# The second half of the latents' columns as one block of 800 columns, 4 of its 16 row pairs in seven products

## The chip, the cores and the metric

The kernel runs on one core of one Trainium2 chip. The metric is the device time of one execution in microseconds (us). The kernel before took 1927.89 us (median of 3 runs, 1927.67 to 1929.81).

## What is computed

One encoder layer on 256 tokens with 4096 features, in float32:

```python
h = rms_norm(x, g_mix)
proj = einsum('bsd,de->bse', h, w_in)
c_q, c_kv, k_rope, gate_a, q_b, k_b, v_b, gate_b = split(proj, split_idx)
q_a = einsum('bsr,re->bse', rms_norm(c_q, g_q_latent), w_uq)
kv = einsum('bsr,re->bse', rms_norm(c_kv, g_kv_latent), w_ukv)
# dense attention on q_a, kv and the rotated k_rope; windowed attention on q_b, k_b, v_b;
# both gated, w_out, residual; then a gated embedding through w_ple and w_ple_gate; a last rms_norm
```

The change concerns the first 1600 columns of `w_in`: 1024 of the query latent `c_q`, 512 of the key and value latent `c_kv`, and 64 of the rotary key `k_rope`. The kernel calls them the latents. After them come 2048 columns of the gate `gate_a`.

## The kernel before

**Products.** The 256 tokens are two tiles of 128, and the 4096 features are 32 row blocks of 128. Each float32 operand is held as a high and a low part, and each product of a 128x128 piece of x with a row block of weights is three matmuls (`mm`, lines 133 to 135: high by high, high by low, low by high). A row block of weights is loaded by SyncE into a buffer `raw` (4 of them, `RAW`), ScalarE writes its high part `hi` (line 115), and VectorE subtracts it for the low part `lo` (line 116).

**Steps.** All products stand in one list `steps`, and the loop at the end of the program goes through it. In round i it emits the loads and conversions of the steps ahead (`fetch`, `convert`), the matmuls of step i, and then one turn of every running task (`advance`). How far conversions go ahead is set by the ring of `hi`/`lo` buffers: a step with the ring `WP` of three buffers has two further steps converted, a step with a longer ring five (line 1470, `tiles`). All engines take their instructions in the order in which they were emitted. A task is a generator; a `yield` ends its turn. `hook(n, f)` calls f ahead of step n.

**The latents (steps 0 to 63).** They are four chunks of 400 columns (line 1159), 16 steps each; a step takes two row blocks, that is 12 matmuls of 400 columns. At the end of a chunk `done_a(i)` scales the two token tiles out of PSUM into `c_tok` (line 335 on VectorE, 337 on ScalarE), squares the columns for the norms on ScalarE (347), and `turn_c` transposes finished groups of 256 columns through PSUM and splits them into `cT` (316, 125, 127). Chunk 3 spawns `latents`, which copies and rotates the rotary key on GpSimd (370, 212 to 215), transposes it (379), and sets the flag `kpe`; its last turn computes the norms and sets the flag `latents`, for which the steps of `w_uq` and `w_ukv` wait. The banks of PSUM are named m0 to m3, s, o, t0 and t1; the chunks use m0/m1 and m2/m3 in turn, and transposes take t0 and t1 in turn (`turn_bank`).

**Blocks.** The first 1024 columns of the gate, and other wide matrices, are a `Block`: two halves of 512 columns by two token tiles. A pair of row blocks is done either plainly (two steps `c` of 12 matmuls, 24 in all), or by a form of Strassen's scheme (four steps `s` of 3, 6, 6 and 6 matmuls, 21 in all) with seven products instead of eight. The latter needs four differences of weights on VectorE (820) and four sums of x for the pair (`add_sums`, 858 with the splits 115 and 116). `weave(fast, lead, trail)` gives the order of the steps: `lead` plain ones, then the pairs spread among plain ones, then `trail` plain ones. After the last `s` the task `mid` (here `gates_mid`) combines four of the eight PSUM banks, and after the last step `done` (`gates_done`) adds the other four. The gate's block is `weave(range(7), 8, 2)`: 7 of 16 pairs in seven products. Its sums, `x0_sums`, come from a task that is spawned at step 24 (line 1224) and makes the sums of one pair in every four turns, with buffers T2 and T3.

At steps 0 to 15 x is loaded, transposed and split; at step 24 the task `rotary_tables` is spawned, which computes angles on VectorE (181 to 197) and their sine and cosine on ScalarE (200 to 203).

Of the kernel before, what the change touches and what calls it, by code (L numbers as in the profile page):

```python
# [18 lines left out]
P = 128  # L19
# [59 lines left out]
def encoder_layer(ctx: ExitStack, tc: tile.TileContext, x, p, positions, g_mix, w_in, g_q_latent, w_uq,  # L79
# [242 lines left out]

    def done_a(i):
        def task(ps):
            if i == 0:
                yield from x_stats()
                for t in range(NT):
                    c_tok.append(slot(f"B{t}", [OFF_GA]))
                qh, ql = slot("B4", [8, S], F32R), slot("B5", [8, S], F32R)
                kv = slot("B6", [2, 4, S], F32R)  # L330
                cT["q"], cT["kv"] = (qh, ql), (kv[:, 0], kv[:, 1])
            for t in range(NT):
                dst = c_tok[t][:, 400 * i:400 * (i + 1)]
                if t:
                    nc.vector.tensor_scalar(dst, ps[t], rx[:, t:t + 1], None, op0=ALU.mult)
                else:
                    nc.scalar.activation(dst, ps[t], AF.Copy, scale=rx[:, t:t + 1])
            yield
            if i == 3:
                spawn(latents())  # L340
            ends = [400 * i, min(400 * (i + 1), Q_LORA + KV_LORA)]
            if ends[0] < Q_LORA < ends[1]:
                ends.insert(1, Q_LORA)
            for lo, hi in zip(ends, ends[1:]):
                c = 4 if lo == Q_LORA else 5 if lo > Q_LORA else i
                for t in range(NT):
                    nc.scalar.activation(junk[:, :hi - lo], c_tok[t][:, lo:hi], AF.Square,
                                         accum_out=sums[:, c, t:t + 1])
                    yield
            while i and ("cT", i - 1) not in flags:  # L350
                yield
            yield from turn_c(((0,), (1, 2), (3,), (4, 5))[i])
            flags.add(("cT", i))
            if i == 3:
                tot = stat(2 * NT)
                q, kv = tot[:, :NT], tot[:, NT:]
                nc.vector.tensor_tensor(q, sums[:, 0], sums[:, 1], op=ALU.add)
                nc.vector.tensor_tensor(kv, sums[:, 4], sums[:, 5], op=ALU.add)
                nc.vector.tensor_tensor(q, q, sums[:, 2], op=ALU.add)
                nc.vector.tensor_scalar(q, q, KV_LORA / Q_LORA, None, op0=ALU.mult)  # L360
                yield from rsqrt_mean(rqkv, tot, KV_LORA)
                nc.vector.tensor_scalar(rqs, rq, (NOPE + ROPE) ** -0.5, None, op0=ALU.mult)
                flags.add("latents")
        return task
# [292 lines left out]
    def d_mid(key, blk):  # L657
        def task():
            tags = D_TAGS[key]
            if len(tags) == 2:  # L660
                d = [slot(b, [NT, 512]) for b in tags]
            else:
                both = slot(tags[0], [2, NT, 512])
                d = [both[:, 0], both[:, 1]]
            D[key] = d
            if key == ("v", 1):
                E["d"] = slot("T5", [2, NT, S])
                nc.gpsimd.dma_start(E["d"], c_dist)
            ps = blk.ps
            sc = [(rxq if key[0] == "q" else rx)[:, t:t + 1] for t in range(NT)]  # L670

            def add(h, t, m, old):
                nc.vector.scalar_tensor_tensor(d[h][:, t], ps[m], sc[t], old, op0=ALU.mult, op1=ALU.add)

            for t in range(NT):
                nc.scalar.activation(d[0][:, t], ps["M1"], AF.Copy, scale=sc[t])
            for t in range(NT):
                add(1, t, "M6", d[0][:, t])
            add(0, 1, "M7", d[1][:, 1])
            add(1, 0, "M5", d[1][:, 0])  # L680
            add(1, 1, "M5", d[0][:, 1])
            flags.add(("mid", key))
            yield
        return task

    def d_done(key, blk):
        def task():
            d = D[key]
            sc = [(rxq if key[0] == "q" else rx)[:, t:t + 1] for t in range(NT)]
            for m, t, h in (("M2", 0, 0), ("X", 1, 1), ("M3", 0, 1), ("M4", 1, 0)):  # L690
                nc.vector.scalar_tensor_tensor(d[h][:, t], blk.ps[m], sc[t], d[h][:, t], op0=ALU.mult, op1=ALU.add)
            if key == ("v", 1):
# [65 lines left out]
    class Step:  # L758
# [4 lines left out]
        def __init__(self, load, split, run, needs=(), frees=0):  # L763
            self.load, self.split, self.run, self.needs, self.frees, self.after = load, split, run, needs, frees, None
            self.ring, self.flag = WP, None

    Q = 512

    class Block:
# [8 lines left out]

        def __init__(self, w, lhs, sums, name, order, needs, tags, tmp, ring):
            self.w, self.lhs, self.sums, self.name, self.needs, self.tmp = w, lhs, sums, name, needs, tmp  # L780
# [6 lines left out]
        def product(self, m, a, b):  # L787
            first = m not in self.ps
            if first:
                self.ps[m] = bank(self.tags[m], [Q])  # L790
            self.left[m] -= 1
            mm(self.ps[m], a, b, first, self.left[m] == 0)

        def load(self, kt):
            r = wp.tile([P, 2, Q], F32, tag="raw", name=f"raw_{kt}", bufs=RAW)
            nc.sync.dma_start(r.rearrange("p a b -> p (a b)"), self.w[kt * P:(kt + 1) * P, :])
            return r
# [14 lines left out]
        def fast_steps(self, j):  # L812
# [9 lines left out]
            def split1(hi, lo):  # L822
                if isinstance(self.tmp, tuple):
                    T.extend(slot(b, [2, Q]) for b in self.tmp)
                else:
                    both = slot(self.tmp, [4, Q])
                    T.extend((both[:, :2], both[:, 2:]))
# [24 lines left out]
    def add_sums(n, pair, dst, tmp, name, out, rest=0, first=0):  # L852
# [3 lines left out]
        def task():  # L856
# [8 lines left out]
            for j in range(first, n):  # L865
# [12 lines left out]
                for _ in range(1 + rest):  # L878
                    yield
        return task()  # L880


# [96 lines left out]
    P4 = {}  # L979
    WIDE_PLE = {(0, 0): "m0", (0, 1): "m1", (1, 0): "t0", (1, 1): "t1"}  # L980

# [175 lines left out]

    for i in range(4):
        add(from_x(400 * i, 400, done_a(i)))
# [20 lines left out]
    def lay(blk, order, mid, done, ple=None, after=(), used={}):  # L1180
# [5 lines left out]
        for i, key in enumerate(shape):  # L1186
            x = next(step[key])
            x.ring = WP + list(after) if after != () and i > last else blk.ring
            if key == "s":
# [64 lines left out]

    tags = EVEN
    for n, key in enumerate((key, i) for i in range(2) for key in "qkv"):
# [15 lines left out]

    tags = EVEN
    for k in range(WIDE_O):
        hook(len(steps), only(*(("t0", "t1"), ("m0", "m1"), ("m2", "m3"))[k]))
        for h in range(2):
# [6 lines left out]
    for c in (6, 7):  # L1283
        hook(len(steps), lambda c=c: (load_res(c), only("t0", "t1")()))
        if c == 7:
            hook(len(steps) + 6, lambda: spawn(x1_sums()))
            hook(len(steps) + 11, lambda: spawn(load_p()))
        add(Chunk(cols(w_out, 512 * c, 512), 32, 512, lhs_y, ("m2", "m3") if c == 6 else ("m0", "m1"), done_o(c), need_y))
    kept = [("B1",), ("B4",), ("B5",), ("B6",), ("B7a", "T6")]
# [6 lines left out]
    for k in range(WIDE):  # L1296
        order = weave(*((range(6), 6, 4) if k == 0 else (range(7), 4, 4)), 2)
        blk = Block(w_ple_gate[:, 1024 * k:1024 * (k + 1)], lhs_x1, x1_s, "x1_sums", order,
                    lambda kt: [("x1T", kt // 4)], LAST, "B6", WP + ["B4"])
# [3 lines left out]
    tail_banks = {6: (("m0", "m1"), ("t0", "t1")), 7: (("m2", "o"), ("s", "m3")), 8: (("m0", "m1"), ("t0", "t1"))}  # L1303

# [83 lines left out]
    def tiles(i, st):  # L1388
# [11 lines left out]
        seen.append(i)  # L1400
        shape = [st.ch.per, st.ch.n] if isinstance(st, Old) else [2, 512]
        if tag == "wp":
# [124 lines left out]
```

## Time and profile before

| | |
|---|---|
| median of 3 runs | 1927.89 us |
| the profiled execution | 1927.64 us |
| its span, first to last instruction | 1925.9 us |
| matmuls and transposes in the trace | 9272 |
| first matmul of the gate's block | 157.20 us |
| VectorE busy from 175 to 231 us (seven-product pairs of the gate's block) | 55.25 of 56 us |

The profile is one execution; its times are microseconds from its span's start. PE is TensorE's matmul, PEld its weight load, DVE VectorE, ACT ScalarE, POOL GpSimd, SP SyncE. A matmul is listed as longer than the distance to the next, since matmuls overlap in the array; the distance from start to start is what one costs. A group's row gives its line, engine, operation, written tile and read tiles, count, busy time and mean ns of one, and the engine's idle time before it. A row of a wait gives the total, the times and the longest.

### The profile page before, as it was taken

Reading aid. Unit: us, or ns where it says so; the run is one execution under the profiler, and the core shown is the slowest. Engines: PE = TensorE matmul, PEld = TensorE weight load, DVE = VectorE, ACT = ScalarE, POOL = GpSimd, SP = SyncE. Lnnn points to the kernel's source line nnn. Section 1 sums busy time; section 2 is a strip of 40 time slices with the busy share of each in tenths; the row PEclk is TensorE's granted clock in tenths of the full one; section 3 lists DMA queues with packets and bytes.
Section 4 is the critical chain, followed back from the end, with each engine's and each line's share of the span. In section 5 each row is a group of like instructions: output and inputs, shape, how many; then the busy total and the mean of one; then the engine's idle time right before and its main releaser. Section 6 shows DMA issues by size and latency. Waiting matters only on the chain.

```text
span 1925.9 us, 25586 instructions
## 1 busy us (share of the span) xinstructions
PE 1909.8 (99%) x9272; PEld 1626.7 (84%) x9272; DVE 1560.8 (81%) x2162; ACT 1101.3 (57%) x1513; POOL 74.5 (4%) x122
## 2 busy tenths in 40 slices
PE   9999999999999999999999999999999999999997
PEld 8998889998888888888888888888888888888887
DVE  7766966665999999999887778889896698989866
ACT  6555555565555555655556666555565456666643
POOL 1001011220000000000000010000000000000000
PEclk9999999999999999999999999999999999999999
DMA  7676655455666666666664456665666656566675
GB/s 251 188 187 198 196 172 144 145 150 162 188 185 209 209 217 197 209 197 196 218 197 139 135 165 218 201 215 174 230 194 217 189 184 218 186 210 204 207 220 176
DMA packets 147342, 370.59 MB, mean 192 GB/s; under 512 B 12020, under 2 KB 45904, under 8 KB 147216
## 3 DMA queue, kind: packets, MB, share of 16 engines
q1 hardware_dynamic: 145584, 363.90, 61.9%
q0 software_dynamic: 1632, 5.05, 0.7%
q8 instruction: 73, 1.20, 0.3%
q14 instruction: 53, 0.43, 0.1%
HBM read 364.72 MB, written 4.19 MB: 192 GB/s over the span
## 4 chain that ended last, share of the span: by engine, by line
PE 94%; DVE 4%; DMA 1%; issue 1%; ACT 1%; SPq 0%; DVEq 0%; ACTq 0%
PE m L134 20%; PE m L135 20%; PE m L133 20%; PE t L134 4%; PE t L135 4%; PE t L133 4%; PE s L134 3%; PE o L134 3%; PE o L135 3%; PE o L133 3%; PE s L135 3%; PE s L133 3%; DVE lo L116 1%; PE t L445 1%; DVE B L820 1%
## 5 line engine op out<-in xcount | busy, mean ns | idle before, releaser
L116 DVE TENSOR_TENSOR lo<-raw,hi 128x1024 fp32r<-128x1024 f32 (+4 forms) x497 | 549.0, 1109 | 227.6 <-ACT hi L115 225.0
L115 ACT ACTIVATE hi<-raw 128x1024 fp32r<-128x1024 f32 (+4 forms) x497 | 478.4, 967 | 365.9 <-PE m L135 181.2
L133 PE MATMUL m<-hi,Ah 128*128 128x512 f32 (+2 forms) x1130 | 429.2, 380 | 0.0
L134 PE MATMUL m<-lo,Ah 128*128 128x512 f32 (+2 forms) x1130 | 424.6, 376 | 0.9 <-DVE lo L116 0.7
L135 PE MATMUL m<-hi,Al 128*128 128x512 f32 (+2 forms) x1128 | 422.3, 374 | 0.0
L134 PEld LDWEIGHTS m<-lo,Ah 128*128 128x128 f32 x1130 | 212.9, 188 | 34.6 <-DVE lo L116 5.0
L135 PEld LDWEIGHTS m<-hi,Al 128*128 128x128 f32 x1128 | 212.3, 188 | 32.8 <-DVE Al L127 0.2
L133 PEld LDWEIGHTS m<-hi,Ah 128*128 128x128 f32 x1130 | 213.0, 188 | 30.1
L133 PE MATMUL m<-hi,B 128*128 128x512 f32 (+1 forms) x420 | 160.4, 382 | 0.0
L134 PE MATMUL m<-lo,B 128*128 128x512 f32 (+1 forms) x420 | 156.8, 373 | 0.2 <-DVE lo L116 0.2
L135 PE MATMUL m<-hi,B 128*128 128x512 f32 (+1 forms) x420 | 156.7, 373 | 0.0
L115 ACT ACTIVATE hi<-B 128x1024 fp32r<-128x1024 f32 x75 | 79.5, 1061 | 79.9 <-DVE B L820 50.3
L116 DVE TENSOR_TENSOR lo<-B,hi 128x1024 fp32r<-128x1024 f32 x75 | 91.6, 1223 | 4.1 <-ACT hi L115 1.8
L135 PEld LDWEIGHTS m<-hi,B 128*128 128x128 f32 x420 | 78.9, 188 | 11.7
L134 PEld LDWEIGHTS m<-lo,B 128*128 128x128 f32 x420 | 79.1, 188 | 11.3 <-DVE lo L116 0.9
L133 PEld LDWEIGHTS m<-hi,B 128*128 128x128 f32 x420 | 79.0, 188 | 10.6
L115 ACT ACTIVATE B<-raw 128x1024 fp32r<-128x1024 f32 (+1 forms) x66 | 60.5, 925 | 45.8 <-DMA raw<-in_w_in_dram 17.4
L820 DVE TENSOR_TENSOR B<-raw,B 128x512 f32<-128x512 f32 x126 | 86.3, 685 | 0.0
L115 ACT ACTIVATE B<-B 128x1024 fp32r<-128x1024 f32 (+1 forms) x60 | 57.4, 957 | 44.4 <-DVE B L820 22.1
L116 DVE TENSOR_TENSOR B<-raw,B 128x1024 fp32r<-128x1024 f32 (+1 forms) x66 | 69.4, 1059 | 13.5 <-ACT B L115 13.2
L116 DVE TENSOR_TENSOR T<-t,T 128x512 fp32r<-128x512 f32 (+1 forms) x65 | 44.4, 683 | 41.6 <-ACT T L115 41.2
L835 DVE TENSOR_TENSOR lo<-raw,hi 128x1024 fp32r<-128x1024 f32 x57 | 69.5, 1219 | 1.9 <-ACT hi L833 1.8
(780 smaller groups left out, 3774.3 us busy)
## 6 DMA issues: line engine op xcount, KB each, us to landing
raw<-in_w_in_dram SPq DMA_DIRECT2D x320, 512.0 KB, 4.1
raw<-in_w_out_dram SPq DMA_DIRECT2D x128, 512.0 KB, 4.4
raw<-in_w_ple_gate_dram SPq DMA_DIRECT2D x128, 512.0 KB, 4.4
raw<-in_w_in_dram SPq DMA_DIRECT2D x63, 400.0 KB, 3.7
raw<-in_w_uq_dram SPq DMA_DIRECT2D x32, 384.0 KB, 3.5
raw<-in_w_ukv_dram SPq DMA_DIRECT2D x16, 512.0 KB, 3.7
T<-in_x_dram SPq DMA_DIRECT2D x7, 512.0 KB, 6.0
T<-in_x_dram POOLq DMA_DIRECT2D x7, 512.0 KB, 8.2
```

Source lines behind the costliest of these rows:

```text
L115: nc.scalar.activation(hi, src, AF.Copy)
L116: nc.vector.tensor_tensor(lo, src, plain(hi), op=ALU.subtract)
L133: nc.tensor.matmul(ps, ah, bh, start=start, stop=False)
L134: nc.tensor.matmul(ps, ah, bl, start=False, stop=False)
L135: nc.tensor.matmul(ps, al, bh, start=False, stop=stop)
L445: nc.tensor.transpose(tp[:, k, t * P:(t + 1) * P], e[:, t, k * P:(k + 1) * P], ident)
L820: nc.vector.tensor_tensor(dst, a, b, op=ALU.subtract)
L835: nc.vector.tensor_tensor(lo, r[1], plain(hi), op=ALU.subtract)
```

## The change

Chunks 0 and 1 stay. The columns 800 to 1599 become one `Block` with halves of 400 columns, `weave(range(4), 8, 4)`: 4 of 16 pairs in seven products, 40 steps (24 plain ones and 16 of the four pairs). Its `mid` and `done` tasks (`late_mid`, `late_done`) call `half_way` and `all_way`, which are the former bodies of `d_mid` and `d_done`. `late_done` then spawns `latents`, transposes the groups 3, 4 and 5 on the banks o and s, squares, and computes the norms. The sums of x are begun at step 17 instead of 24, one pair in every three turns, with buffers T4 and B7b. The block has a fourth buffer pair, (T6, T5), in its ring, and (T2, T3) after its last pair. The gate's block takes its banks in the order of `follow(EVEN)`, and from there on m0/m1 and m2/m3 are exchanged. `EVEN` is (m0, m1, s, o, m2, m3, t0, t1), and a block's banks stand in the order M2, X, M3, M4, M1, M5, M6, M7.

```diff
@@ turn_c
             split_rows(*(q[:, o:o + 2] for q in cT[key]), tp, G[key][:, o:o + 2])
-            yield
+            if b < 3:
+                yield
@@ done_a: the part for i == 3, the turns (3,) and (4, 5) and the norms go; new tasks
+    def late(h, t):
+        return c_tok[t][:, 800 + 400 * h:1200 + 400 * h]
...
+    def late_mid(blk):
+        def task():
+            half_way(blk.ps, [rx[:, t:t + 1] for t in range(NT)], late)
+            yield
+        return task
...
+    def late_done(blk):
+        def task():
+            all_way(blk.ps, [rx[:, t:t + 1] for t in range(NT)], late)
+            yield
+            assert ("cT", 1) in flags
+            spawn(latents())
+            yield from turn_c((3, 4, 5))
+            for c, lo, hi in ((2, 800, Q_LORA), (4, Q_LORA, 1200), (5, 1200, Q_LORA + KV_LORA)):
+                yield from square(c, lo, hi)
...
+    def half_way(ps, sc, d):
+
+        def add(h, t, m, old):
+            nc.vector.scalar_tensor_tensor(d(h, t), ps[m], sc[t], old, op0=ALU.mult, op1=ALU.add)
+
+        for t in range(NT):
+            nc.scalar.activation(d(0, t), ps["M1"], AF.Copy, scale=sc[t])
+        for t in range(NT):
+            add(1, t, "M6", d(0, t))
+        add(0, 1, "M7", d(1, 1))
+        add(1, 0, "M5", d(1, 0))
+        add(1, 1, "M5", d(0, 1))
+
+    def all_way(ps, sc, d):
+
+        for m, t, h in (("M2", 0, 0), ("X", 1, 1), ("M3", 0, 1), ("M4", 1, 0)):
+            nc.vector.scalar_tensor_tensor(d(h, t), ps[m], sc[t], d(h, t), op0=ALU.mult, op1=ALU.add)
...
-    for i in range(4):
+    for i in range(2):
         add(from_x(400 * i, 400, done_a(i)))
...
-    hook(24, lambda: spawn(add_sums(7, x_pair, z0_dst, ("T2", "T3"), "x0_sums", x0_s, 2)))
+    hook(17, lambda: spawn(add_sums(7, x_pair, z0_dst, ("T4", "B7b"), "x0_sums", x0_s, 1)))
...
+    order = weave(range(4), 8, 4)
+    blk = Block(w_in[:, 800:1600], lhs_x, x0_s, "x0_sums", order, lambda kt: (), EVEN, ("T2", "T3"),
+                WP + [("T6", "T5")], 400)
+    lay(blk, order, late_mid(blk), late_done(blk), after=[("T2", "T3")])
+    hook(len(steps), only("o", "s"))
     order = weave(range(7), 8, 2)
-    blk = Block(w_in[:, OFF_GA:OFF_GA + 1024], lhs_x, x0_s, "x0_sums", order, lambda kt: (), EVEN, ("T2", "T3"),
+    blk = Block(w_in[:, OFF_GA:OFF_GA + 1024], lhs_x, x0_s, "x0_sums", order, lambda kt: (), follow(EVEN), ("T2", "T3"),
                 WP + [("T5", "T6")])
     lay(blk, order, gates_mid(blk), gates_done(blk))
+    hook(len(steps), only("t0", "t1"))
+    M = M[::-1]
```

More of the change, by code (lines that the diff above doesn't have):

```diff
@@ L338, in task @@
             yield
[L339 to L349, printed above, removed]
+            yield from square(i, 400 * i, 400 * (i + 1))
@@ L350, in task @@
             while i and ("cT", i - 1) not in flags:
                 yield
-            yield from turn_c(((0,), (1, 2), (3,), (4, 5))[i])
+            yield from turn_c(((0,), (1, 2))[i])
             flags.add(("cT", i))
[L354 to L363, printed above, removed]
+        return task
@@ L668, in task @@
                 nc.gpsimd.dma_start(E["d"], c_dist)
[L669 to L681, printed above, removed]
+            half_way(blk.ps, [(rxq if key[0] == "q" else rx)[:, t:t + 1] for t in range(NT)], lambda h, t: d[h][:, t])
             flags.add(("mid", key))
@@ L688, in task @@
             d = D[key]
-            sc = [(rxq if key[0] == "q" else rx)[:, t:t + 1] for t in range(NT)]
-            for m, t, h in (("M2", 0, 0), ("X", 1, 1), ("M3", 0, 1), ("M4", 1, 0)):
-                nc.vector.scalar_tensor_tensor(d[h][:, t], blk.ps[m], sc[t], d[h][:, t], op0=ALU.mult, op1=ALU.add)
+            all_way(blk.ps, [(rxq if key[0] == "q" else rx)[:, t:t + 1] for t in range(NT)], lambda h, t: d[h][:, t])
             if key == ("v", 1):
@@ L777, in encoder_layer, with __init__ @@
         NAMES = "M2", "X", "M3", "M4", "M1", "M5", "M6", "M7"
-        def __init__(self, w, lhs, sums, name, order, needs, tags, tmp, ring):
+        def __init__(self, w, lhs, sums, name, order, needs, tags, tmp, ring, q=Q):
+            self.q = q
             self.w, self.lhs, self.sums, self.name, self.needs, self.tmp = w, lhs, sums, name, needs, tmp
@@ L823, in split1 @@
                 if isinstance(self.tmp, tuple):
-                    T.extend(slot(b, [2, Q]) for b in self.tmp)
+                    T.extend(slot(b, [2, self.q]) for b in self.tmp)
                 else:
-                    both = slot(self.tmp, [4, Q])
+                    both = slot(self.tmp, [4, self.q])
                     T.extend((both[:, :2], both[:, 2:]))
@@ L1271, in encoder_layer @@
         add(ch)
-    tags = EVEN
+    tags = LAST
     for k in range(WIDE_O):
-        hook(len(steps), only(*(("t0", "t1"), ("m0", "m1"), ("m2", "m3"))[k]))
+        hook(len(steps), only(*(("t0", "t1"), ("m2", "m3"), ("m0", "m1"))[k]))
         for h in range(2):
```

33 lines of the change are left out of this document (24 added, 9 removed).

## The prediction

> **What bounds the kernel now.** I read the page first, then the waits of TensorE, then the stretches of the changed stage.
>
> ```profile
> span 1925.9 us, 25586 instructions
> PE 1909.8 (99%) x9272; PEld 1626.7 (84%) x9272; DVE 1560.8 (81%) x2162; ACT 1101.3 (57%) x1513; POOL 74.5 (4%) x122
> PEclk9999999999999999999999999999999999999999
> PE 94%; DVE 4%; DMA 1%; issue 1%; ACT 1%; SPq 0%; DVEq 0%; ACTq 0%
> ```
>
> TensorE is busy for 99% of the span, at the full granted clock in all 40 slices, and 94% of the chain that ended last is TensorE. The busy share alone does not say that nothing is lost, because a matmul's end is modelled. The waits say it:
>
> ```profile
> PE m L1456 <- DVE junk L1450: 1.5, 1, 1.5
> PE m L134 <- DVE lo L116: 0.9, 5, 0.2
> PE t L270 <- DMA T<-in_x_dram: 0.9, 1, 0.9
> ```
>
> Apart from the start, matmuls waited for a low part five times, 0.9 us in all. So the time is the number of matmuls by their distance, and a change pays if it removes matmuls and brings no wait. The stages that matter are these:
>
> ```profile
> core 0: us, PE busy (x) PEld busy (x) DVE busy (x) ACT busy (x) POOL busy (x), PEclk, DMA share, GB/s
> 46.00:86.00 40.00, 40.00 (x226) 39.91 (x225) 29.00 (x69) 22.34 (x38) 0.00 (x0) 1.00 0.65 184
> 86.00:155.00 69.00, 68.99 (x386) 68.51 (x385) 45.76 (x71) 35.74 (x57) 0.00 (x0) 1.00 0.71 192
> 175.00:231.00 56.00, 56.00 (x246) 45.52 (x245) 55.25 (x80) 33.05 (x35) 0.00 (x0) 1.00 0.65 202
> ```
>
> The second row is nearly all of chunks 2 and 3, which the change replaces: VectorE has 23 us to spare there. The third row is the seven-product part of the gate's block: VectorE is at 55.25 of 56 us, so that block is the narrow place behind the change.
>
> **What goes from TensorE.** A pair in seven products is 21 matmuls against 24. Four pairs remove 4 x 3 = 12 matmuls of 400 columns; the instruction lists of the two programs agree (12 fewer of 128x400, the same transposes). One costs the distance of starts:
>
> ```profile
> 119.81 0.35 PE L133 MATMUL m<-hi,Ah 128*128 128x400 f32 x1
> 124.88 0.34 PE L134 MATMUL m<-lo,Ah 128*128 128x400 f32 x1
> ```
>
> These are the first and the last of 29 matmuls in a row, 28 distances: 5.07 / 28 = 0.181 us. **12 x 0.181 = 2.17 us less.**
>
> The Trainium skill, in "TensorE: Matmul & The Clock Gate", section "Back-to-back issue gap", gives N / 2.4 + 2.5 ns for an isolated matmul, 169 ns at 400, and about 131 ns at N = 512 for a stream with weight loads. The sum would be 12 x 0.169 = 2.03 us by the first, and under 12 x 0.131 = 1.6 us by the second (estimates from that page). The trace has 0.181 us for 400 columns in just such a stream, so it agrees with neither, and least with the second.
>
> **What VectorE gains in work.** Rows for its prices, all of before:
>
> ```profile
> L116 DVE TENSOR_TENSOR lo<-raw,hi 128x800 fp32r<-128x800 f32 x43 | 42.5, 990 | 28.8 <-ACT hi L115 28.8
> L116 DVE TENSOR_TENSOR lo<-raw,hi 128x1024 fp32r<-128x1024 f32 x3 | 3.7, 1226 | 2.7 <-ACT hi L115 2.7
> L335 DVE TENSOR_SCALAR B<-m,st 128x400 f32<-128x400 f32 x3 | 1.9, 629 | 0.2 <-PE m L135 0.2
> 200.55 0.69 DVE L820 TENSOR_TENSOR T<-raw 128x512 f32<-128x512 f32 x1
> 201.15 0.68 DVE L820 TENSOR_TENSOR T<-raw,raw 128x512 f32<-128x512 f32 x1
> 208.27 0.69 DVE L820 TENSOR_TENSOR T<-raw 128x512 f32<-128x512 f32 x1
> 575.50 2.19 DVE L673 SCALAR_TENSOR_TENSOR B<-t,st,B 128x512 f32<-128x512 f32 x3
> ```
>
> Instructions in a row overlap by about 0.09 us (starts 0.60 us apart at a length of 0.69). A column costs (1226 - 990) / 224 = 1.05 ns. So from start to start a difference of 400 columns costs 0.60 - 112 x 0.00105 = 0.48 us, a low part of 400 the same, one of 800 0.90 us. A scaled addition out of PSUM costs 2.19 / 3 = 0.73 at 512, so 0.61 us at 400 (estimates from these rows). A pair in seven products takes 4 x 0.48 + 0.48 + 3 x 0.90 = 5.1 us of VectorE, against 1.8 us plain: 13.2 us more for four. Evictions are nine scaled additions instead of two (line 335, about 0.54): 4.4 us more. That is 17.6 us on an engine with 23 us free in the stage, and the sums of five pairs leave it besides.
>
> Locally: between two pairs the order is three plain steps and one pair. TensorE needs 57 x 0.181 = 10.3 us for that, VectorE 5.1 + 3 x 0.9 = 7.8 us. In the gate's block the same account is 7.72 us of VectorE (208.27 - 200.55) against 33 matmuls. So the new block hides its work with 2.5 us per group, and I charge **nothing**. If that cover were gone, the price would be as in the gate's block, below: 0.2 us a pair, under 1 us for four.
>
> ScalarE converts 1200 columns more per pair (a high part of 400 and one of 800), some 5 us in all, and has 33 us free in the stage. SyncE's list has the same 32 loads of 400 KB at the same places, so nothing is queued differently there; the DMA engines are busy for 0.71 of the stage.
>
> **The crowd at steps 24 to 31.** The sums begin seven steps earlier, beside the rotary tables.
>
> ```profile
> 74.67 0.98 DVE L116 TENSOR_TENSOR lo<-raw,hi 128x800 fp32r<-128x800 f32 x1
> 75.57 2.04 DVE L191 SCALAR_TENSOR_TENSOR T<-T 128x64 f32<-128x64 f32 x8
> 70.67 0.69 DVE L858 TENSOR_TENSOR T<-Ah,Al 128x512 f32<-128x512 f32 x1
> 71.40 1.02 DVE L858 TENSOR_TENSOR T<-T 128x128 f32<-128x128 f32 x4
> 81.92 0.63 ACT L115 ACTIVATE B<-T 128x512 fp32r<-128x512 f32 x1 [1.32 <-DVE T L858]
> 82.57 1.28 ACT L200 ACT_TABLE_LOAD   x1
> 84.47 1.62 ACT L115 ACTIVATE hi<-raw 128x800 fp32r<-128x800 f32 x2
> 86.05 0.34 PE L133 MATMUL m<-hi,Ah 128*128 128x400 f32 x1
> 86.40 0.45 PE L134 MATMUL m<-lo,Ah 128*128 128x400 f32 x1
> 86.69 0.34 PE L135 MATMUL m<-hi,Al 128*128 128x400 f32 x1
> ```
>
> Before, the ScalarE part of one pair's sums (81.92, waiting for VectorE) stood ahead of the table load (1.28 us) in step 29; the high part behind it came at 84.47, and TensorE lost (86.69 - 86.05) - 2 x 0.181 = 0.28 us. In the new program no sum's part stands ahead of the table load in that step, so I take the **0.28 us** off. What is late next is VectorE: in step 26 the sums of pair 3 (0.73 + 0.94 us) now stand between two low parts together with the eight operations of line 191 (1.96 us). From the low part of step 28 to the end of that of step 29 this is 0.90 + 1.67 + 1.96 + 0.90 = 5.4 us, where two buffers ahead allow 3 x 2.17 = 6.5 us, less the 1 us in which ScalarE makes the high part. The margin is about 0.1 us at steps 29 and 30. I charge **0.1 us**; bounds 0 and 1.7 us (the whole of a sum, 0.73 + 0.94 us, outside the margin).
>
> **The gate's block.** Its waits are VectorE's deficit:
>
> ```profile
> 203.34 0.39 PE L133 MATMUL m<-T,Ah 128*128 128x512 f32 x1
> 203.63 0.50 PE L134 MATMUL m<-T,Ah 128*128 128x512 f32 x1
> 203.97 0.39 PE L135 MATMUL m<-T,Al 128*128 128x512 f32 x1
> 173.77 0.87 DVE L127 SCALAR_TENSOR_TENSOR B<-t,gT,B 128x256 fp32r<-128x256 f32 x2
> 174.89 0.68 DVE L820 TENSOR_TENSOR T<-raw 128x512 f32<-128x512 f32 x1
> 186.08 0.39 PE L135 MATMUL t<-hi,B 128*128 128x512 f32 x1
> 189.94 0.39 PE L134 MATMUL s<-lo,Ah 128*128 128x512 f32 x1
> ```
>
> From 186.08 to 189.94 are 17 distances: 0.227 us at 512 columns. At 203 TensorE lost 0.63 - 2 x 0.227 = 0.18 us; 33 x 0.227 = 7.49 us against VectorE's 7.72 us gives 0.2 us a pair, so it is the deficit, once the conversions ahead are used up. Three of the five waits above are of this kind, some 0.5 us. In the new program the last transpose's splits (173.77, 0.8 us) come two steps earlier and no longer stand before the first difference (174.89). VectorE enters with 0.8 us in hand, about what the pairs lack. The added evictions (four of 0.61 us) and two further splits (0.8 us) fall into the eight plain steps before, 8 x 12 x 0.227 = 21.8 us with 8 x 1.14 = 9.1 us of low parts. Against it: four more squares on ScalarE among the first pairs, and the norms come later. I take **0.3 us** off; bounds 0.5 less and 0.5 more.
>
> **After it** TensorE's list is the same with banks renamed, and six conversions in all move by a place or so in VectorE's list because the rings stand at another position. I charge nothing, bounds -0.3 and +0.5 us.
>
> **Sum:** -2.17 - 0.28 + 0.1 - 0.3 = -2.65 us, on the profiled execution's 1927.64 us: 1925.0 us. Its median is 0.25 us above that, so 1925.2 us.
>
> **Rivals.**
>
> *The new work eats the gain.* The crowd costs its 1.7 us, the four pairs wait 0.2 us each, the gate's block 0.5 us more, and the moved conversions cost 0.5 us: -2.17 + 3.5 = +1.3, which is 1929.2 us by the median; with half of these costs it is 1927.5. For it speaks that VectorE is near its limit on both sides of the new block; against it that each term needs its own margin to fail.
>
> *Slower: TensorE stands at the first transposes of the second half.* They are in its queue after one step of the gate's block, 12 x 0.227 = 2.7 us, and read what `all_way` writes; the whole queue waits behind them. The last of the four evictions can start only after the block's last matmul and takes 0.61 us, so the cover holds until VectorE is some 2 us behind. Were it behind by all the conversions ahead (five of the gate's block, 5 x 1.14) and the five additions of `half_way` (3.1), 8.8 us, the wait would be 6.8 us and the time 1927.9 - 2.2 + 6.8 = 1932.5 us. It decides from 10.3 us of VectorE per group on, against my 7.8: only then does VectorE fall behind at all. The rotary key is another queue there, but a safe one:
>
> ```profile
> 157.51 0.41 POOL L370 COPY T<-B 128x64 f32<-128x64 f32 x2 [151.04 <-ACT B L337]
> 161.66 1.61 POOL L215 TENSOR_TENSOR T<-T,T 128x256 f32<-128x256 f32 x1
> ```
>
> GpSimd needs 163.27 - 157.51 = 5.8 us, and the rotary key's transposes stand in TensorE's list five steps, 13.6 us, after the block's end.
>
> *The change does not do what it says.* The list of instructions shows the 12 matmuls gone; chance nil.
>
> **How the numbers follow.** The forecast has 78%, the eaten gain 14%, the slower one 4%, and 4% is left for more than I count (other waits going too, under 1924 us). About 0.2%, 3.9 us, is what a measurement of this kernel can tell from no change: forecast and eaten gain both lie within it, but for 1% of the forecast. So faster 5%, same 91%, slower 4%. The forecast's own range is 1924.3 to 1926.8, from the terms' better and worse bounds together with the runs' spread; taking in part of the eaten gain, 1924.2 to 1927.5.
>
> **What would show it.** Right: no wait at TensorE over 0.4 us between 10 and 300 us, 12 fewer matmuls of 400 columns, the first matmul of the gate's block at about 154.8 us (157.20 - 2.17 - 0.28 + 0.1), no wait at step 32 behind the table load, and fewer waits in the gate's pairs. Wrong: waits for `lo` in the new block, at its evictions (transposes on o and s), or shifts of more than 0.5 us after the gate's block.

## The result, and the profile after

| | before | after |
|---|---|---|
| median of 21 runs each | 1927.45 us (1926.14 to 1929.81) | 1929.93 us (1928.8 to 1931.78) |
| the profiled execution | 1927.64 us | 1930.17 us |
| its span | 1925.9 us | 1928.4 us |

The ratio after to before is 1.0014, with a 95% interval of 1.0008 to 1.0019. The forecast was 1925.2 us in a range of 1924.2 to 1927.5. So 2.7 us were expected to go and 2.5 us came.

The page of after: the span, TensorE's line, the granted clock, and the shares of the chain that ended last.

```profile
span 1928.4 us, 25605 instructions
PE 1908.9 (99%) x9260; PEld 1623.0 (84%) x9260; DVE 1575.7 (82%) x2193; ACT 1104.2 (57%) x1521; POOL 75.5 (4%) x122
PEclk9999999999999999999999999999999999999998
PE 91%; DVE 6%; DMA 1%; issue 1%; ACT 1%; SPq 0%; DVEq 0%; ACTq 0%
```

The 12 matmuls are gone (9272 to 9260), the granted clock is at 9 tenths or more in every slice but the last (8), and TensorE's share of the chain went from 94% to 91%, VectorE's from 4% to 6%. VectorE holds TensorE up somewhere. The waits of TensorE in after say where (us in total, times, the longest):

```profile
PE m L133 <- DVE B L901: 1.8, 1, 1.8
PE m L134 <- DVE lo L116: 1.5, 8, 0.3
PE m L134 <- DVE T L116: 0.5, 1, 0.5
PE m L133 <- ACT Ah L125: 0.5, 1, 0.5
```

The first row is new and a single wait: TensorE stood for line 901, which is `all_way`. The waits for low parts (line 116) were 0.9 us in all; the second and third row make 2.0, and one for a low part in a buffer B adds 0.2. The last row is at the very start, which the change does not touch.

Not every loss is a row of that table, so I use one more number. **TensorE's excess** is the sum, over all its instructions of a stretch, of the distance to the next start less the median distance of that size in the same execution (0.227 us at 512 columns, 0.180 at 400). The stretch from 0 to 50 us varies from one execution to the next (2.7 to 6.1 us in the runs below, with no edit there), so the later stretches are compared.

| excess, us | whole span | 0 to 50 | 50 to 100 | 100 to 150 | 150 to 200 | 200 to 250 | 500 to 600 |
|---|---|---|---|---|---|---|---|
| before | 15.3 | 3.7 | 0.68 | 0.31 | 0.16 | 0.61 | 1.34 |
| after | 19.95 | 3.4 | 0.69 | 0.43 | 2.27 | 0.65 | 4.17 |

The excess grew by 4.6 us; 4.6 - 2.17 for the 12 matmuls is the 2.5 us. The new block (86 to 154 us) lost nothing. Nearly all of it came in two places: 2.1 us among the first seven-product pairs of the gate's block, and 2.8 us between 500 and 600 us, of which 2.0 lie at 585 us. That is the end of the block of `q0`, where that of `k0` begins, 430 us behind the end of the new block.

**The place at 585 us.** VectorE in after (start, length, operation; in brackets its idle time before it), and then TensorE:

```profile
581.38 0.68 DVE L116 TENSOR_TENSOR B<-raw,B 128x512 fp32r<-128x512 f32 x1
585.07 1.22 DVE L116 TENSOR_TENSOR lo<-raw,hi 128x1024 fp32r<-128x1024 f32 x1 [3.00 <-ACT hi L115]
586.21 1.40 DVE L901 SCALAR_TENSOR_TENSOR B<-m,st,B 128x512 f32<-128x512 f32 x2
```

```profile
584.94 0.39 PE L135 MATMUL m<-B,Al 128*128 128x512 f32 x1
587.10 0.47 PE L133 MATMUL m<-B,Ah 128*128 128x512 f32 x1 [1.77 <-DVE B L901]
```

The same place on VectorE in the kernel before, where line 691 is what became line 901:

```profile
581.26 0.68 DVE L116 TENSOR_TENSOR lo<-raw,hi 128x512 fp32r<-128x512 f32 x1
581.86 1.40 DVE L691 SCALAR_TENSOR_TENSOR B<-m,st,B 128x512 f32<-128x512 f32 x2
...
584.50 1.22 DVE L116 TENSOR_TENSOR B<-raw,B 128x1024 fp32r<-128x1024 f32 x1
```

Before, the four evictions of `all_way` follow at once on 581.26 and the next low part comes behind them. After, that low part stands ahead of them. It cannot start until ScalarE has its high part, and ScalarE waits for the load:

```profile
583.97 1.06 ACT L115 ACTIVATE hi<-raw 128x1024 fp32r<-128x1024 f32 x1 [6.24 <-DMA raw<-in_w_in_dram]
```

So VectorE is idle for 3.00 us with four evictions behind it that could run, and TensorE needs the bank that they empty.

**The gate's first pairs.** TensorE in after:

```profile
186.07 0.39 PE L133 MATMUL m<-T,Ah 128*128 128x512 f32 x1
187.01 0.50 PE L134 MATMUL m<-T,Ah 128*128 128x512 f32 x1 [0.55 <-DVE T L116]
...
191.61 0.50 PE L134 MATMUL m<-lo,B 128*128 128x512 f32 x1 [0.18 <-DVE lo L116]
...
195.68 0.50 PE L134 MATMUL m<-lo,Ah 128*128 128x512 f32 x1 [0.17 <-DVE lo L116]
```

VectorE in after: a gap at 174, and the first and last of the norms' 17 small operations (the groups with `st`):

```profile
173.47 0.68 DVE L116 TENSOR_TENSOR lo<-raw,hi 128x512 fp32r<-128x512 f32 x1
176.49 1.23 DVE L116 TENSOR_TENSOR lo<-raw,hi 128x1024 fp32r<-128x1024 f32 x1 [2.33 <-ACT hi L115]
...
182.38 0.15 DVE L373 TENSOR_TENSOR st<-st 128x2 f32<-128x2 f32 x1
...
190.26 0.17 DVE L378 TENSOR_SCALAR st<-st 128x2 f32<-128x2 f32 x1
```

And the norms in the kernel before:

```profile
177.83 0.15 DVE L357 TENSOR_TENSOR st<-st 128x2 f32<-128x2 f32 x1
...
185.03 0.17 DVE L362 TENSOR_SCALAR st<-st 128x2 f32<-128x2 f32 x1
```

From the start of the gate's block (157.20 before, 154.37 after) the norms begin 20.6 us in before and 28.0 us in after. Two things are thus different there: a gap in VectorE's work and a later place of the norms.

### The profile page after: what moved, and what is told of

It reads as the page before. It is cut to its first block, busy times and chain, and to the rows that moved or that the text cites. A ratio compares the mean times of both kernels' runs of the same rounds, so it can differ in the third digit from the quotient of the medians.

```text
span 1928.4 us, 25605 instructions
## 1 busy us (share of the span) xinstructions
PE 1908.9 (99%) x9260; PEld 1623.0 (84%) x9260; DVE 1575.7 (82%) x2193; ACT 1104.2 (57%) x1521; POOL 75.5 (4%) x122
## 4 chain that ended last, share of the span: by engine, by line
PE 91%; DVE 6%; DMA 1%; issue 1%; ACT 1%; SPq 0%; DVEq 0%; ACTq 0%
PE m L134 19%; PE m L135 19%; PE m L133 19%; PE t L135 4%; PE t L133 4%; PE t L134 4%; PE s L134 3%; PE o L134 3%; PE o L135 3%; PE o L133 3%; PE s L135 3%; PE s L133 3%; DVE lo L116 2%; DVE B L823 1%; PE t L461 1%
## 5 line engine op out<-in xcount | busy, mean ns | idle before, releaser
L116 DVE TENSOR_TENSOR lo<-raw,hi 128x1024 fp32r<-128x1024 f32 (+3 forms) x473 | 522.3, 1110 | 206.7 <-ACT hi L115 203.9
L115 ACT ACTIVATE hi<-raw 128x1024 fp32r<-128x1024 f32 (+3 forms) x473 | 455.7, 969 | 341.9 <-PE m L135 155.4
L133 PE MATMUL m<-hi,Ah 128*128 128x512 f32 (+2 forms) x1033 | 395.1, 382 | 0.5 <-ACT Ah L125 0.5
L134 PE MATMUL m<-lo,Ah 128*128 128x512 f32 (+2 forms) x1033 | 391.1, 379 | 1.6 <-DVE lo L116 1.4
L135 PE MATMUL m<-hi,Al 128*128 128x512 f32 (+2 forms) x1031 | 388.3, 377 | 0.0
L133 PE MATMUL m<-hi,B 128*128 128x512 f32 (+2 forms) x431 | 164.6, 382 | 0.0
L134 PE MATMUL m<-lo,B 128*128 128x512 f32 (+2 forms) x431 | 160.9, 373 | 0.2 <-DVE lo L116 0.2
L135 PE MATMUL m<-hi,B 128*128 128x512 f32 (+2 forms) x431 | 160.9, 373 | 0.0
L116 DVE TENSOR_TENSOR T<-t,T 128x512 fp32r<-128x512 f32 x64 | 43.9, 687 | 41.6 <-ACT T L115 41.2
L838 DVE TENSOR_TENSOR lo<-raw,hi 128x1024 fp32r<-128x1024 f32 (+1 forms) x58 | 70.0, 1206 | 2.2 <-ACT hi L836 2.2
L133 PE MATMUL m<-B,Ah 128*128 128x512 f32 (+1 forms) x178 | 66.2, 372 | 1.8 <-DVE B L901 1.8
```

Source lines behind the costliest of these rows:

```text
L115: nc.scalar.activation(hi, src, AF.Copy)
L116: nc.vector.tensor_tensor(lo, src, plain(hi), op=ALU.subtract)
L133: nc.tensor.matmul(ps, ah, bh, start=start, stop=False)
L134: nc.tensor.matmul(ps, ah, bl, start=False, stop=False)
L135: nc.tensor.matmul(ps, al, bh, start=False, stop=stop)
L838: nc.vector.tensor_tensor(lo, r[1], plain(hi), op=ALU.subtract)
```

## The experiments

**First theory: the ring's position.** `tiles` deals the buffers of the `hi`/`lo` ring out in turn (`at[0]`). The new block has 40 steps where two chunks had 32, so the gate's block begins at index 2 of the ring instead of 1. From there on a conversion can find its buffer in another turn, and so stand elsewhere in the engines' lists. That would explain the low part ahead of the evictions at 585 us, and perhaps the gap at 174. **Rivals:** the norms' later place takes VectorE from the gate's first pairs; or the new block itself (sums, loads, banks) costs the time. The median of the kernel before lay between 1927.23 and 1927.32 us in these runs.

**1. The ring set back.** One line in `tiles`; the change stays.

```diff
         ring = st.ring
+        at[0] = {72: 1}.get(i, at[0])
         n = at[0] % len(ring)
```

> The changed kernel with one edit: at its first step of the gate's block the position in the ring of hi/lo buffers is set to the one that the kernel before has there (index 1 instead of 2). No instruction is added or taken away; conversions in and after the gate's block are emitted as far ahead of their steps as in the kernel before. Ring theory: both new stalls go, the 1.8 us wait of TensorE at the start of the k0 stage (for B of all_way's line) and the waits of 0.3 to 0.7 us in the gate's first pairs, so 1929.9 - 4.6 = 1925.3 us, ratio to the kernel before about 0.9988. Rival, the norms that come later take VectorE from the gate's pairs: the wait at k0 goes but the gate's 2 us stay, about 1927.5. Rival, the new block itself (its loads, its sums) costs the time: no change, 1929.9.

Measured: 1926.47 us (1925.8 to 1928.93), ratio to the kernel before 0.9997 (0.9988 to 1.0006). The excess at 500 to 600 us is 1.34, as before the change; at 150 to 200 us it is 1.69, of 2.27. So the ring holds the whole of the loss at 585 us, but only 0.6 us of that at the gate. Both expectations missed the total by about 1 us, from either side. (The profiled execution is the longest of its runs; 2.7 us of it were lost ahead of 50 us, where the two programs are the same.)

**2. One conversion held back.** Only the low and high part of step 243 are kept two steps longer; the ring stays as the change has it.

```diff
+        if i == 243 and ran[0] < 239:
+            return None
```

> The changed kernel with one conversion held back: that of step 243, the last but few of q0, is emitted four steps ahead as in the kernel before and not six. Ring theory: VectorE then has the evictions of all_way ahead of the low part that waits for its load, the 1.77 us wait at 587 us goes, and the time falls by 1.5 to 2.8 us, to about 1927.5; the waits in the gate's block (about 2 us more than before) stay. Rival, the evictions are late for another reason (banks exchanged, VectorE simply full there): the wait stays, 1929.9.

Measured: 1927.40 us (1927.02 to 1928.05), 2.5 us under the changed kernel; excess at 500 to 600 us 1.76. VectorE in this run:

```profile
581.40 0.69 DVE L116 TENSOR_TENSOR B<-raw,B 128x512 fp32r<-128x512 f32 x1
582.00 1.41 DVE L901 SCALAR_TENSOR_TENSOR B<-m,st,B 128x512 f32<-128x512 f32 x2
...
584.64 1.22 DVE L116 TENSOR_TENSOR lo<-raw,hi 128x1024 fp32r<-128x1024 f32 x1
```

The evictions are in front again, and the wait for line 901 is gone. In VectorE's order this run differs from the changed kernel in this one instruction alone, so its place costs the 2.5 us. (What is left over the 1.34 us of before is a wait for another low part, at 551 us.) The excess at 150 to 200 us stays at 2.28.

**3. The ring shifted in the kernel before.** Nothing of the change is in it.

```diff
         ring = st.ring
+        at[0] = {64: 2}.get(i, at[0])
         n = at[0] % len(ring)
```

> The kernel before with one edit: at the first step of the gate's block the ring stands at index 2 instead of 1, as it does in the changed kernel. Nothing of the change itself is in it. Ring theory: the stall of about 1.8 us at k0 and about 2 us of waits in the gate's pairs appear here too, so 1927.5 + 4 to 4.6 = 1931.5 to 1932 us, ratio 1.002. Rivals (norms, new block, exchanged banks): 1927.5, ratio 1.000; if only one of the two stalls belongs to the ring, about 1929.5.

Measured: 1929.87 us (1928.68 to 1930.08), ratio 1.0012 (1.0003 to 1.002). VectorE has the order of the changed kernel:

```profile
582.77 0.69 DVE L116 TENSOR_TENSOR B<-raw,B 128x512 fp32r<-128x512 f32 x1
585.07 1.23 DVE L116 TENSOR_TENSOR lo<-raw,hi 128x1024 fp32r<-128x1024 f32 x1 [1.62 <-ACT hi L115]
586.22 1.41 DVE L691 SCALAR_TENSOR_TENSOR B<-m,st,B 128x512 f32<-128x512 f32 x2
```

A number that says where a ring stands is enough to cost 2.6 us. The excess rose by 1.0 us at 150 to 200 and by 1.5 at 500 to 600; about half of what theory one wanted, so something else stands behind the gate's loss in the changed kernel.

**4. The norms earlier.** The ring stays as the change has it. The squares are emitted in three turns, beside the transposes, so that the norms come about six turns sooner.

```diff
-            yield from turn_c((3, 4, 5))
+            spawn(turn_c((3, 4, 5)))
             for c, lo, hi in ((2, 800, Q_LORA), (4, Q_LORA, 1200), (5, 1200, Q_LORA + KV_LORA)):
-                yield from square(c, lo, hi)
+                for _ in square(c, lo, hi):
+                    pass
+                yield
```

> The changed kernel with the squares and the norms of the latents emitted about six turns earlier, beside the transposes of the last groups (the squares three to a turn). The ring stays as the change has it. Norms rival: the gate's first pairs lose their waits, -2 us, 1927.9. Ring theory: VectorE's idle time of 2.3 us at 174 us stays, since a conversion ahead is missing there and not time, so no more than -0.7 us, 1929.2 to 1930; the wait at k0 of 1.77 us stays under both.

Measured: 1927.64 us (1926.67 to 1929.76), 2.3 us under the changed kernel. The excess at 150 to 200 us is 0.23. The norms rival was right for the gate, and my first theory falls there. VectorE:

```profile
174.36 0.16 DVE L229 SCALAR_TENSOR_TENSOR st<-st 128x4 f32<-128x4 f32 x1
...
174.95 0.17 DVE L380 TENSOR_SCALAR st<-st 128x2 f32<-128x2 f32 x1
176.31 1.23 DVE L116 TENSOR_TENSOR lo<-raw,hi 128x1024 fp32r<-128x1024 f32 x1 [1.19 <-ACT hi L115]
```

The gap is still there, but now the norms lie ahead of it and partly in it, and the pairs behind are free of them. The wait for `all_way` stays (1.5 us; line numbers are those of each run's own kernel, so it is line 903 here).

**5. The norms later in the kernel before.** Ring and all else as before.

```diff
             if i == 3:
+                for _ in range(6):
+                    yield
                 tot = stat(2 * NT)
```

> The kernel before with one edit: the norms' 17 small operations on VectorE are held back by six turns, about 7 us, so that they stand among the gate's first pairs as in the changed kernel. Ring and everything else as before. If the norms' place costs the time at the gate: waits of 0.3 to 0.7 us there and 1927.3 + 1.3 to 2.0 = 1928.6 to 1929.3 us. If it costs only together with the ring or the new block: 1927.3.

Measured: 1929.24 us (1929.04 to 1931.63), ratio 1.0013 (1.0004 to 1.0022): 2.0 us. VectorE, and then TensorE:

```profile
177.60 1.23 DVE L837 TENSOR_TENSOR lo<-raw,hi 128x1024 fp32r<-128x1024 f32 x1 [0.25 <-ACT hi L835]
...
180.37 1.23 DVE L116 TENSOR_TENSOR lo<-T,hi 128x1024 fp32r<-128x1024 f32 x1 [0.94 <-ACT hi L115]
...
185.13 1.22 DVE L116 TENSOR_TENSOR lo<-raw,hi 128x1024 fp32r<-128x1024 f32 x1 [0.60 <-ACT hi L115]
...
188.61 0.15 DVE L359 TENSOR_TENSOR st<-st 128x2 f32<-128x2 f32 x1
```

```profile
194.83 0.50 PE L134 MATMUL m<-lo,Ah 128*128 128x512 f32 x1 [0.45 <-DVE lo L116]
...
196.64 0.50 PE L134 MATMUL m<-lo,Ah 128*128 128x512 f32 x1 [0.84 <-DVE lo L116]
```

This is the mechanism in the open. Early in the pairs VectorE has gaps, here 0.25 + 0.94 + 0.60 = 1.79 us, because conversions have run as far ahead as their buffers allow: the high part that VectorE waits for starts each time only at the end of a matmul of line 135, after 1.66, 1.71 and 0.73 us in which ScalarE was idle. In the kernel before the norms fill these gaps. Put later, they leave the gaps empty and stand where VectorE has no time left, and TensorE pays 2.00 - 0.16 = 1.84 us of excess at 150 to 200 us. The six turns came to about 12 us and not to the 7 that were expected: the norms begin 32.6 us into the gate's block here, 28.0 in the changed kernel and 20.6 in the kernel before. So this run shows the mechanism, and not the exact price of the changed kernel's place.

**6. Both repairs.** The edits of experiments 1 and 4 together.

> The changed kernel with both edits: the ring's position at the gate's block as in the kernel before, and the norms about six turns earlier. In the runs so far the ring alone took TensorE's excess at 150 to 200 us from 2.27 to 1.69 us, and the norms alone to 0.23. Theory of two causes (norms for most of the gate's waits, ring for the wait at k0): the gate's excess is about 0.2, the k0 wait is gone, and the time is 1926.5 - 1.5 = 1925.0 us, which is the forecast's value, ratio 0.9988. Rival, the two edits overlap so that the norms' bring nothing once the ring is set: 1926.5.

Measured: 1924.93 us (1923.98 to 1926.3), ratio 0.9988 (0.9979 to 0.9997). TensorE's waits:

```profile
PE m L1488 <- DVE junk L1482: 1.5, 1, 1.5
PE m L134 <- DVE lo L116: 1.1, 6, 0.2
PE t L270 <- DMA T<-in_x_dram: 0.9, 1, 0.9
PE m L133 <- ACT Ah L125: 0.5, 1, 0.5
```

Excess 0.23 at 150 to 200 and 1.30 at 500 to 600 us. This is the time that the forecast gave to the change, and the theory of two causes holds.

**7. Both costs in the kernel before.** The edits of experiments 3 and 5 together.

> The kernel before with both costs of the change and nothing of its gain: the ring at index 2 from the gate's block on, and the norms held back by six turns. Apart they measured +2.6 and +2.0. If they are two causes that add: 1927.3 + 4.6 = 1931.9 us, and the change itself (this run to the changed kernel, 1929.9) would be worth -2.0 to -2.4. If a wait at the gate only moves what follows towards its load and shortens the wait at k0: 1930 to 1931.

Measured: 1930.98 us (1930.0 to 1931.56), ratio 1.0018 (1.0009 to 1.0027): 3.75 us, not 4.6. They do not add: the excess at 150 to 200 us is 2.19 us, against 1.13 with the ring and 2.00 with the norms alone. The time lies in the second range that was expected, but not for its reason: at 500 to 600 us the excess is 2.96, no less than in experiment 3 (2.81); what overlaps lies at the gate. The changed kernel has 4.17 there. The wait at 585 us is thus not a constant of the order; with the same order TensorE stood there for

```profile
588.00 0.47 PE L133 MATMUL m<-B,Ah 128*128 128x512 f32 x1 [0.59 <-DVE B L693]
```

instead of 1.77 us. The low part that VectorE waits for starts at 585.97 here; in experiment 3 and in the changed kernel it starts at 585.07 in both, though TensorE had come to this place at 586.33 in the one and 584.94 in the other. So the same order costs more where TensorE is earlier against the load. The load itself is issued as soon as a low part on VectorE has freed its buffer `raw`: at 575.61 us in the kernel before, 579.15 in the changed kernel, 580.54 in experiment 3 and 581.24 here. It took 5.1, 4.7, 3.3 and 3.5 us from issue to landing. The ring thus acts twice: it holds back the low part that frees the buffer, which makes the load later, and it puts the next low part ahead of the evictions. The first alone costs little, since in experiment 2 the load is issued at 579.18 and lands after 4.2 us, and the 2.5 us are not lost. Why the load took 4.7 us in one run and 3.3 in another is not shown.

**8. The new block without its added tile.** On experiment 6: the ring of the new block is `WP` alone, and (T2, T3) do not follow its last pair.

```diff
-                WP + [("T6", "T5")], 400)
-    lay(blk, order, late_mid(blk), late_done(blk), after=[("T2", "T3")])
+                WP, 400)
+    lay(blk, order, late_mid(blk), late_done(blk))
```

> As the run with ring and norms, without the tile that the change added to the new block's ring (T6, T5) and without (T2, T3) behind its last pair: conversions of the new block go two steps ahead and not five. The forecast had the new block's VectorE work covered by 2.5 us per group and did not count on the added tile. If the cover alone carries it: no waits from 86 to 154 us, 1924.9. If the conversions further ahead are what hides the differences of weights: waits in the new block's pairs, 0.5 us or more each, 1927 us or more.

Measured: 1926.89 us (1926.07 to 1928.99): 2.0 us more than with the tile. The excess at 100 to 150 us is 2.59 (0.43 with it). VectorE and TensorE:

```profile
146.68 1.84 DVE L890 SCALAR_TENSOR_TENSOR B<-t,st,B 128x400 f32<-128x400 f32 x3
148.43 1.17 DVE L890 SCALAR_TENSOR_TENSOR B<-m,st,B 128x400 f32<-128x400 f32 x2
149.52 2.79 DVE L116 TENSOR_TENSOR lo<-raw,hi 128x800 fp32r<-128x800 f32 x3
```

```profile
150.55 0.45 PE L134 MATMUL m<-lo,Ah 128*128 128x400 f32 x1 [1.24 <-DVE lo L116]
```

The five additions of `half_way` take 3 us in one piece, and the low part for the next step stands behind them.

**9. (T2, T3) without the added tile.** As 8, but `after=[("T2", "T3")]` is kept.

> As the run with ring and norms, without the added tile (T6, T5), but with (T2, T3) behind the last pair kept. In the run without both, TensorE waited 1.4 us at 149 us, behind the five additions of the block's half-way point on VectorE, and about 0.9 us in the pairs. If those are two covers: the wait at 149 us goes and the pairs' waits stay, 1924.9 + 0.9 = 1925.8 us. If the tile in the pairs is what matters for both: 1926.9.

Measured: 1927.58 us (1927.09 to 1928.07), excess at 100 to 150 us 2.84. The wait at 149 us does not go; it is now the 1.2 us for a low part in T:

```profile
PE m L134 <- DVE T L116: 1.2, 1, 1.2
```

So (T2, T3) alone give no cover, and my picture of two covers was wrong: the added pair of buffers is needed in both places. Whether it would do without (T2, T3) was not run.

**10. The sums at step 24.** On experiment 6: the earlier start of the sums undone.

```diff
-    hook(17, lambda: spawn(add_sums(7, x_pair, z0_dst, ("T4", "B7b"), "x0_sums", x0_s, 1)))
+    hook(24, lambda: spawn(add_sums(7, x_pair, z0_dst, ("T4", "B7b"), "x0_sums", x0_s, 2)))
```

> As the run with ring and norms, with the sums of x begun at step 24 and one pair in every four turns as in the kernel before (buffers T4 and B7b kept). The forecast put the earlier start at -0.28 us (the wait behind the table of ScalarE) and +0.1 (VectorE's crowd): without it 1924.9 + 0.2 = 1925.1 us, with a wait of 0.3 us near step 32. If the first pair of the new block needs its sums sooner than they come: waits before 120 us and more than 1926.

Measured: 1925.55 us (1924.95 to 1927.44), 0.6 us more. The wait behind the table load is back: 0.28 us at 86 us. But two of 0.11 us at 79 and 82 us, which the earlier start has, are gone, so the stretch from 50 to 100 us has 0.7 us of excess either way. The loss is elsewhere; from 100 to 150 us the excess of the profiled execution is 1.65 us, against 0.43:

```profile
123.37 0.45 PE L134 MATMUL m<-lo,B 128*128 128x400 f32 x1 [0.38 <-DVE lo L116]
...
124.92 0.45 PE L134 MATMUL t<-T,B 128*128 128x400 f32 x1 [0.19 <-DVE T L116]
```

Sums begun later still run while the new block's first pairs do (VectorE makes them at 106, 113 and 120 us here), and take VectorE from them.

**11. Six pairs** instead of four, on experiment 6; the index is set at step 76, where the gate's block then begins.

```diff
-    order = weave(range(4), 8, 4)
+    order = weave(range(6), 8, 4)
```

> As the run with ring and norms, with 6 instead of 4 pairs of the new block in seven products (6 matmuls of 400 columns fewer; the ring's position set for the block's 44 steps). If the new block has VectorE to spare as the forecast worked out (7.8 us of VectorE per 10.3 us of TensorE at three plain steps to a pair): 1925.0 - 1.1 = 1923.9 us. If VectorE is the bound there as soon as pairs stand closer: 1925 or more, with waits of TensorE between 86 and 154 us.

Measured: 1923.24 us (1922.84 to 1925.14), ratio 0.9982 (0.9973 to 0.9991), the fastest of all. The excess at 100 to 150 us is 0.47: the two further pairs cost no wait. The medians differ by 1.7 us and the matmuls are worth 1.1; the runs' ranges do not tell these apart.

**12. Seven pairs**, in the same way (index set at step 78).

> As the run with ring and norms, with 7 pairs in seven products (9 matmuls of 400 columns fewer than with 4). By the matmuls alone 1925.0 - 1.6 = 1923.4 us. With one or two plain steps to a pair VectorE needs 5.1 + 0.9 us or more against 33 x 0.181 = 6.0 us of TensorE, so waits of some 0.2 us a pair are possible: up to 1924.8 us.

Measured: 1925.37 us (1924.82 to 1926.94). The excess at 100 to 150 us is 2.56, 2.1 more than with four, against 1.6 us of matmuls saved. The largest wait:

```profile
115.86 0.45 PE L134 MATMUL m<-lo,Ah 128*128 128x400 f32 x1 [0.55 <-DVE lo L116]
```

Between six and seven pairs VectorE becomes the limit of the new block, with a dearer end than the 0.2 us a pair that I had put down.

## Why the prediction was wrong

**The matmuls, -2.17: as forecast.** 12 are gone, their distance in the changed kernel is 0.180 us as before, and with both other costs taken out the time is 2.3 us under the kernel before (experiment 6). No run has the 12 matmuls as its only difference.

**The new block at nothing: right, but by a cover that the forecast did not name.** It argued from VectorE's sums of work, 7.8 us per 10.3 us of TensorE, and put under 1 us on the loss of the cover. The work is indeed hidden, but by the added buffers: without them 2.0 us are lost (experiment 8) with the same work, twice the price that the forecast gave to a lost cover.

**The table's wait, -0.28, and the crowd, +0.1: together 0.** The wait went as said. The crowd cost two waits of 0.11 us. The prediction's place for the first matmul of the gate's block was 154.8 us:

```profile
154.37 0.39 PE L133 MATMUL m<-hi,Ah 128*128 128x512 f32 x1
```

It came 0.4 us earlier still, which is no gain: four transposes of about 0.11 us each stood ahead of it before and stand in the gate's block now.

**The gate's block, -0.3 with bounds of 0.5: the first step that failed.** The forecast wrote "the norms come later" as a point against it, and gave it no price. The price could be read: 17 operations, from 177.83 to 178.91 and in three further pieces of 0.46 to 0.65 us, 2.65 us of VectorE in a stage where it is busy for 55.25 of 56 us. They had cost so little because they lay in the gaps before the pairs had used up the conversions ahead. Moved out of them in the kernel before they cost 2.0 us (experiment 5), and moved back in the changed kernel they give 2.3 us back (experiment 4). The gain that the forecast counted here was there beneath: over the 75 us from the block's first matmul on, the excess is 0.74 us before, 2.90 after, and 0.22 with both repairs, and the three waits of 0.2 us in the later pairs are gone. (The windows of 150 to 200 and 200 to 250 us do not show it, because 0.36 us of the next stage move into the second.) No run tells whether the splits that come earlier bring this, as the forecast had it, or the norms, which with the repair lie ahead of the pairs.

**"After it", at nothing with bounds of -0.3 and +0.5: the second step that failed, and the larger.** It named the very thing, conversions that "move by a place or so in VectorE's list because the rings stand at another position", and gave 0.5 us as the most that they could cost, without a working. But the one at step 243 moved ahead of four evictions for which TensorE waits, and itself waits for a load: 2.5 us (experiment 2). In the kernel before the ring alone cost 2.6 us, 1.5 of them between 500 and 600 us (experiment 3). Against experiment 1, seven low parts stand elsewhere in VectorE's order of the changed kernel, each of them four to six places away and not "a place or so". One more of the seven stands ahead of four evictions of `all_way`, at 990 us; its high part was there, VectorE went from 989.29 to 991.64 us without a gap, and TensorE has no wait there. So what a moved instruction costs was set by what it waited for, 3.00 us of idle VectorE at the one place and none at the other, and not by its length of 1.22 us.

**The rivals.** The eaten gain had a mechanism for the gate, VectorE's work, and for what follows, the moved conversions, and its full price of 1929.2 us came nearest to the result. That nearness is luck: 2.5 of its 3.5 us, the crowd and the four pairs, did not come, and the two terms that did, 0.5 us each, were 2.1 and 2.8. The slower rival, TensorE standing at the first transposes on o and s, did not occur: no such wait is in the trace. Of the prediction's own signs, the shift of over 0.5 us behind the gate's block showed, and so did a wait of over 0.4 us in the gate's pairs (0.55 at 187.01).

**The range.** Its upper end, 1927.5, is lower than the forecast's own worse bounds allow: 1.6 + 0.5 + 0.5 us over 1925.2 are 1927.8. Even that lies under the 1929.93 measured. And 3.9 us was too large for what a measurement here can tell from no change: with 21 runs each the 2.5 us are clear (1.0008 to 1.0019).

**What stays open:** with one and the same order, the kernel loses 1.5 us between 500 and 600 us in experiment 3 (2.81 - 1.34) and 2.8 us in the changed kernel (4.17 - 1.34). TensorE comes 1.4 us later in experiment 3 and the load lands at the same time, which is the difference; why the load, issued 1.4 us later there, was not later to land is open. Open is also how much of the ring's share at the gate (0.6 to 1.0 us with the norms where they were, none once they are early) is the gap at 174 us.

## What to carry to other kernels

When a change alters the number of steps ahead of a shared ring of buffers, follow the ring through the whole program: list for each engine which instructions change order, and price each by what the moved one waits for and by who stands behind it. Small work on a full engine is free only in that engine's gaps, so when it moves, look for the gap that it leaves and the one that it lands in. And where conversions ahead hide a stage's work, a sum of busy time does not tell whether the buffers let them go far enough: try the number of buffers as well.

## What the runs showed that I had not expected

A ring index, one number without any instruction of its own, is worth 2.6 us in 1927 (experiment 3, ratio 1.0012, 1.0003 to 1.002), and its largest effect showed some 430 us behind the place where it was set. And one more pair of buffers hid what a sum of VectorE's work said was hidden already: 2.0 us in a block of 68 us in which VectorE had, by that sum, a quarter of its time to spare (experiments 8 and 9).
